# Four sums of weight blocks moved from VectorE to GpSimd in a two-layer diffusion trunk

## The chip, the cores and the metric

The kernel runs on one core of one Trainium2 chip. The metric is device time in microseconds of one execution, the median of several; less is better. The engines of the core are TensorE (PE: matmuls; PEld: its weight loads), VectorE (DVE), ScalarE (ACT), GpSimd (POOL) and SyncE (SP), which issues the DMAs.

## What is computed

Two layers of a diffusion backbone over 640 tokens (512 latent tokens on a grid, 128 context tokens) of 1024 channels. Each layer is a half-step SwiGLU FFN, a mixing stage (neighbourhood attention, pooling, short convolution, merged by gates) and a second FFN. Each of them starts with an RMSNorm, shifted and scaled by an adaLN projection of a conditioning vector. So there are four FFNs, and the change is in them:

```python
def swiglu(h, w_gate, w_up, w_down):
    return (jax.nn.silu(h @ w_gate) * (h @ w_up)) @ w_down

def trunk_layer(x, mod, lp, attend):
    h = modulate(rmsnorm(x, lp['g_ffn1']), m[0], m[1])
    x = x + 0.5 * m[2] * swiglu(h, lp['w_ffn1_gate'], lp['w_ffn1_up'], lp['w_ffn1_down'])
    ...
    x = x + m[5] * (merged @ lp['w_out'])
    h = modulate(rmsnorm(x, lp['g_ffn2']), m[6], m[7])
    x = x + 0.5 * m[8] * swiglu(h, lp['w_ffn2_gate'], lp['w_ffn2_up'], lp['w_ffn2_down'])
    return x, k, v
```

## The kernel before

**Splitting.** All matmuls are made of two-part numbers: a weight block or operand is copied to a rounded high part (hi, on ACT, line 310, tile wh for weights) and the rest is subtracted (lo, on VectorE, line 313, tile wl). One product of 128 channels is three matmuls: hi x hi, lo x hi and hi x lo (mm3, lines 305 to 307). `split` does this for activations (nhi, nlo; gh, gl for the gated activations), `w_part` for weights.

**Units.** An FFN has 22 columns of 128 hidden channels, in chunks of 8, 8 and 6. The first two columns of an FFN are multiplied as they are (`whole`); each of the other 20 is a *unit*: gate and up weights (with the two halves of the tokens) are multiplied in seven products of a Strassen-like scheme in the place of eight. A unit's weights come by three DMAs into three buffers of the ring RAW (four buffers): raw with both halves of the gate, a11 with half of up in its lower 512 columns, a12 with the other half in its upper 512. Four sums of 128x512 blocks complete them (`add`, line 386):

- sum 1: upper part of a11 = the two halves of raw
- sum 2: lower part of sm = the two parts of a11
- sum 3: upper part of sm = lower part of sm + upper part of a12
- sum 4: lower part of a12 = lower part of a11 + upper part of raw

Then a11, sm, a12 (1024 wide) and the lower part of raw (512 wide) are split into weight tiles of the ring HL (four pairs). sm is the one buffer of the ring SUM. TensorE takes the four tiles in this order: a11 for products B11 and T1, sm for T2 and B22, a12 for T3 and `prod_b`, raw for T4. Each product is four times three matmuls of 320 columns. Three results are saved from their bank by ACT (`hold`, a copy f<-b, line 310), three are added to a saved one by VectorE (`plus`, line 901), one of which, n22 after T3, must be done before T4 may write its bank. Then come silu, f x f (line 873) and the split into gh and gl. After a chunk's units the down weights are multiplied (`dn`, whole 1024-wide tiles without sums), and VectorE adds the result to x (line 799).

**Starts of an FFN.** `norm_b` makes the operand's rows: squares (line 651) and their sum on ACT and VectorE, the power -1/2 on GpSimd (line 671), scaling (line 695, 740) and split of each row of 128 channels. TensorE follows the rows with the `whole` columns. Then the forms T1 to T4 of the operand are computed, 1280 wide, and split (nhi, nlo). The gated activations gh and gl reuse memory that these forms are read from.

**adaLN.** The projections for later norms are made on VectorE in the meantime, as products of 512 with a running sum (line 573), and paced by the weight tiles that TensorE is done with.

**Order.** The order of all instructions is written out beforehand by a planner (`Sched`): processes ask for an engine with a cost (`DVE(n)`, `POOL(n)`, `ACT(n)`, `PE(n, m)`), for buffers of a ring, or for events, and the planner gives an engine to whichever request can start first, by its priority if two can. Each engine then runs its own list in that order; waits between engines are semaphores that follow the data. What a process asks for between two instructions, such as the HL slot between sums 1 and 2, places its next instruction in the plan, but is no wait of that instruction on the chip.

The lists that the change touches are those of VectorE and GpSimd (lines 386, 400, 408, 410 and 417). GpSimd otherwise runs the power of the norms (line 671), some memsets, and small products of the mixing stage (lines 1252, 1258, 1259, 1269, 1332).

Of the kernel before, what the change touches and what calls it, by code (L numbers as in the profile page):

```python
# [11 lines left out]
ALU = mybir.AluOpType  # L12
# [167 lines left out]
def DVE(n, m=1):  # L180
    return ("dve", 0.1 + m * 0.05 + n / 960)


def POOL(n):
    return ("pool", 0.16 + n * 0.0021)
# [82 lines left out]
def body(ctx: ExitStack, tc: tile.TileContext, a, outs):  # L268
    nc = tc.nc
# [100 lines left out]
    def w_part(hl, i, src, n, nk):  # L370

        hi, lo = [t[:, :n] for t in hl]
        yield ACT(n)
        copy(hi, src)
        yield DVE(n)
        sub(lo, src, hi)
        cnt["split"] += 1
        S.set(w_ev[i], (i, hl, *[t.rearrange("p (k c) -> p k c", k=nk) for t in (hi, lo)]))

    def w_split():  # L380
        def nxt():
            tile_no[0] += 1
            return tile_no[0] - 1

        def add(out, in0, in1):
            nc.vector.tensor_tensor(out=out, in0=in0, in1=in1, op=ALU.add)

        prio = S.cur.prio
        for i0, nk, ncol in pieces:
            raw = yield raw_ev[i0]  # L390
            if nk:
                hl = yield HL
                yield from w_part(hl, nxt(), raw[:, :nk * ncol], nk * ncol, nk)
                S.give(RAW, raw)
                continue
            a11 = yield raw_ev[i0 + 1]
            a12 = yield raw_ev[i0 + 2]
            lo, hi = slice(0, 512), slice(512, 1024)

            yield DVE(512)  # L400
            add(a11[:, hi], raw[:, hi], raw[:, lo])
            hl = yield HL
            p1 = S.spawn(w_part(hl, nxt(), a11, 1024, 8), prio)

            def part_b():

                sm = yield SUM
                yield DVE(512)
                add(sm[:, lo], a11[:, hi], a11[:, lo])
                yield DVE(512)  # L410
                add(sm[:, hi], sm[:, lo], a12[:, hi])
                hl = yield HL
                return sm, S.spawn(w_part(hl, nxt(), sm, 1024, 8), prio)

            def part_c():

                yield DVE(512)
                add(a12[:, lo], a11[:, lo], raw[:, hi])
                hl = yield HL
                return S.spawn(w_part(hl, nxt(), a12, 1024, 8), prio)  # L420

            sm, p2 = yield from part_b()
            p3 = yield from part_c()
            yield p1
            S.give(RAW, a11)
            yield p2
            S.give(SUM, sm)

            hl = yield HL
            yield from w_part(hl, nxt(), raw[:, lo], 512, 4)  # L430
            S.give(RAW, raw)
            yield p3
            S.give(RAW, a12)
# [1531 lines left out]
    def main():  # L1965
        S.spawn(prep(), 0)
        es = ExitStack()
        fp = es.enter_context(tc.tile_pool(name="first", bufs=1))
        for j in range(4):
            S.give(FIRST, fp.tile([128, 2048], F32, name=f"wf{j}"))  # L1970
        nt_ev = Ev()
        xe, ops = start_norms(0, 0, nt_ev)
        S.set(
            nt_ev,
            (
                [fp.tile([128, 4, 320], F32, name=f"nf{j}") for j in range(4)],
                [fp.tile([128, 4, 320], F32R, name=f"b{s}") for s in "hl"],
            ),
        )
        done = S.spawn(ada_first(first), 1)  # L1980
        S.spawn(load(xe), 2)
        S.spawn(w_split(), w_prio)
        close = closer(es, [done])
        for l in range(L):
            more = l + 1 < L
            op, _ = yield from ffn(l, 0, ops, close, lambda: start_norms(l, 1), False, l == 0)
            ops, close = yield from mix(l, op, lambda ev: start_norms(l, 2, ev))
            ops, close = yield from ffn(l, 1, ops, close, (lambda ev: start_norms(l + 1, 0, ev)) if more else None, more, False)
# [89 lines left out]
```

## Time and profile before

| | |
|---|---|
| runs shown | 2751.22, 2753.77, 2752.55 us |
| median | 2752.55 us |
| profiled execution | 2751.35 us |
| its span in the profile | 2749.6 us |
| TensorE busy | 2704.8 us (98% of the span) |
| VectorE busy | 2092.8 us (76%) |
| ScalarE busy | 1276.6 us (46%) |
| GpSimd busy | 125.6 us (5%) |

The profile is one execution. Times are microseconds from the start of the span unless marked ns. A row of the timeline is start, duration, engine, line of the kernel, operation, what is written <- what is read, shape, xcount where neighbours are merged, and in brackets the idle time of the engine before it and what ended it. Instructions of one engine are pipelined, so the next can start a little before the last has ended. Matmul durations overlap; two matmuls of 320 columns start some 0.147 us apart.

### The profile page before, as it was taken

How to read it: one execution, taken by the hardware profiler on the slowest of the kernel's cores; microseconds unless marked ns; L12 is line 12 of the kernel's file. 1: busy time of each engine (PE TensorE's matmuls, PEld its weight loads, DVE VectorE, ACT ScalarE, POOL GpSimd, SP SyncE). 2: the span in 40 equal slices, each digit the busy share in tenths (PEclk: the TensorE clock that was granted, in tenths of full speed). 3: DMA queues.
4: the chain of work that ended last, by engine and by line, in shares of the span. 5: the costliest groups of instructions: out<-in, count | busy, mean ns of one | idle time of the engine just before them, and what ended most of it. 6: DMA issues, size and time to landing. Idle time of an engine off the chain costs nothing.

```text
span 2749.6 us, 48276 instructions
## 1 busy us (share of the span) xinstructions
PE 2704.8 (98%) x19068; PEld 2679.2 (97%) x19068; DVE 2092.8 (76%) x4164; ACT 1276.6 (46%) x2312; POOL 125.6 (5%) x217
## 2 busy tenths in 40 slices
PE   7999999999999999999999999999999999999999
PEld 6999999999999999999999999999999999999999
DVE  7998976776677799988688686768766768847564
ACT  5525244895322463443464252558943225524342
POOL 0000000530000000000000000004200000000000
PEclk9999999999999999999999999999999999999999
DMA  5453523232444235353324233323234441222222
GB/s 220 142 166 102 167 95 109 89 99 74 134 135 149 75 97 167 108 160 112 104 77 138 78 109 111 98 91 108 71 97 143 138 135 47 77 92 77 93 70 85
DMA packets 123186, 304.91 MB, mean 111 GB/s; under 512 B 15696, under 2 KB 23888, under 8 KB 121936
## 3 DMA queue, kind: packets, MB, share of 16 engines
q1 hardware_dynamic: 122960, 301.83, 33.9%
q8 instruction: 149, 2.44, 0.4%
q14 instruction: 77, 0.63, 0.1%
HBM read 298.11 MB, written 3.67 MB: 110 GB/s over the span
## 4 chain that ended last, share of the span: by engine, by line
PE 92%; ACT 3%; DVE 3%; issue 1%; DMA 1%; POOL 0%; SPq 0%; DVEq 0%; POOLq 0%
PE b L305 29%; PE b L307 29%; PE b L306 29%; ACT nhi L310 1%; PE b L1466 1%; ACT t L719 1%; DVE wl L313 1%; DMA wf<-in_wm_dram 1%; PE b L1378 1%; PE b L1377 0%; PE b L1373 0%; DVE nlo L313 0%; PE b L1372 0%; PE b L1395 0%; DVE t L695 0%
## 5 line engine op out<-in xcount | busy, mean ns | idle before, releaser
L305 PE MATMUL b<-nhi,wh 128*128 128x320 f32 (+2 forms) x3584 | 1111.8, 310 | 8.0 <-ACT nhi L310 4.0
L306 PE MATMUL b<-nhi,wl 128*128 128x320 f32 (+2 forms) x3584 | 1107.2, 309 | 0.2 <-DVE wl L313 0.2
L307 PE MATMUL b<-nlo,wh 128*128 128x320 f32 (+2 forms) x3520 | 1087.9, 309 | 3.3 <-DVE nlo L313 3.2
L310 ACT ACTIVATE wh<-raw 128x1024 fp32r<-128x1024 f32 (+2 forms) x472 | 457.7, 970 | 557.2 <-PE b L307 475.7
L305 PEld LDWEIGHTS b<-nhi,wh 128*128 128x128 f32 x3584 | 673.6, 188 | 12.3 <-ACT nhi L310 6.5
L306 PEld LDWEIGHTS b<-nhi,wl 128*128 128x128 f32 x3584 | 673.7, 188 | 2.6 <-DVE wl L313 1.8
L307 PEld LDWEIGHTS b<-nlo,wh 128*128 128x128 f32 x3520 | 661.6, 188 | 6.8 <-DVE nlo L313 6.7
L313 DVE TENSOR_TENSOR wl<-raw,wh 128x1024 fp32r<-128x1024 f32 (+2 forms) x472 | 525.5, 1114 | 169.0 <-ACT wh L310 167.5
L305 PE MATMUL b<-gh,wh 128*128 128x320 f32 (+2 forms) x1424 | 440.9, 310 | 0.0
L307 PE MATMUL b<-gl,wh 128*128 128x320 f32 (+2 forms) x1424 | 440.1, 309 | 0.0
L306 PE MATMUL b<-gh,wl 128*128 128x320 f32 (+2 forms) x1424 | 439.8, 309 | 0.0
L306 PEld LDWEIGHTS b<-gh,wl 128*128 128x128 f32 x1424 | 267.8, 188 | 0.3
L305 PEld LDWEIGHTS b<-gh,wh 128*128 128x128 f32 x1424 | 267.7, 188 | 0.3
L307 PEld LDWEIGHTS b<-gl,wh 128*128 128x128 f32 x1424 | 267.8, 188 | 0.3
L799 DVE SCALAR_TENSOR_TENSOR x<-b,mh,x 128x128 f32<-128x128 f32 (+3 forms) x288 | 117.3, 436 | 160.2 <-PE b L307 160.1
L573 DVE CUSTOM_DVE_ANT_0 junk<-wm,cs,part 128x512 bf16<-128x512 f32 x256 | 191.7, 749 | 21.0 <-ACT cs L539 9.1
L310 ACT ACTIVATE f<-b 128x320 f32<-128x320 f32 x240 | 104.6, 438 | 216.2 <-PE b L307 214.0
L573 DVE CUSTOM_DVE_ANT_0 junk<-wm,cs,bm 128x512 bf16<-128x512 f32 x256 | 191.4, 748 | 14.0 <-DMA wm<-in_wmod_dram 7.7
L901 DVE TENSOR_TENSOR f<-f,b 128x320 f32<-128x320 f32 x240 | 112.2, 483 | 107.6 <-PE b L307 102.7
L305 PE MATMUL b<-wh,nhi 128*128 128x256 f32 x480 | 138.2, 288 | 0.4 <-DVE nhi L313 0.4
L306 PE MATMUL b<-wh,nlo 128*128 128x256 f32 x480 | 134.5, 280 | 2.1 <-DVE nlo L313 2.1
L307 PE MATMUL b<-wl,nhi 128*128 128x256 f32 x480 | 134.2, 280 | 0.0
(209 smaller groups left out, 3355.1 us busy)
## 6 DMA issues: line engine op xcount, KB each, us to landing
raw<-in_w_dram SPq DMA_DIRECT2D x280, 512.0 KB, 3.4
wm<-in_wmod_dram SPq DMA_DIRECT2D x256, 256.0 KB, 3.1
raw<-in_w_dram SPq DMA_DIRECT2D x160, 256.0 KB, 2.8
raw<-in_w_dram SPq DMA_DIRECT2D x32, 384.0 KB, 3.1
B<-in_rpb_dram SPq DMA_DIRECT2D x16, 640.0 KB, 4.1
wf<-in_wm_dram SPq DMA_DIRECT2D x8, 1024.0 KB, 12.0
cs<-in_crow_dram SPq DMA_DIRECT2D x20, 256.0 KB, 4.9
x<-in_xT_dram SPq DMA_DIRECT2D x4, 640.0 KB, 8.7
```

Of the source, the lines that this page charges most:

```text
L305: nc.tensor.matmul(out, lhsT=l2[0], rhs=r2[0], start=first, stop=False, skip_group_check=more)
L306: nc.tensor.matmul(out, lhsT=l2[1], rhs=r2[0], start=False, stop=False, skip_group_check=more)
L307: nc.tensor.matmul(out, lhsT=l2[0], rhs=r2[1], start=False, stop=last, skip_group_check=more)
L310: nc.scalar.activation(out=out, in_=in_, func=AF.Copy, scale=scale)
L313: nc.vector.tensor_tensor(out=out, in0=in0, in1=in1, op=ALU.subtract)
L573: nc.vector.tensor_tensor_reduce(out=junk, in0=t, in1=cs[:, g, 512 * hf:512 * hf + 512] if wide else cs[:, g], scale=1.0, scalar=start, op ...
L719: nc.scalar.activation(out=t[:, c0:c1], in_=t[:, c0:c1], func=AF.Identity, scale=gs[:, 1, d, g:g + 1], bias=M[:, 24 + d, g:g + 1])
L799: nc.vector.scalar_tensor_tensor(out=x[:, d, s], in0=bank[:, c0:c1], scalar=col[:, d, g:g + 1], in1=x[:, d, s], op0=ALU.mult, op1=ALU.add)
L901: nc.vector.tensor_tensor(out=t, in0=t, in1=bank[:, :320], op=ALU.add)
L1378: nc.tensor.matmul(out, lhsT=v, rhs=pt[1][:, :n], start=False, stop=last)
L1466: nc.tensor.transpose(bank[:, 128 * i:128 * i + 128], P[h, j][:, 128 * s:128 * s + 128], ident)
```

## The change

The helper `add` issues its tensor_tensor on GpSimd in the place of VectorE, and the four requests to the planner ask for GpSimd. Nothing else is changed: the same additions of the same blocks in the same program order.

```diff
@@ -383,7 +383,7 @@
         def add(out, in0, in1):
-            nc.vector.tensor_tensor(out=out, in0=in0, in1=in1, op=ALU.add)
+            nc.gpsimd.tensor_tensor(out=out, in0=in0, in1=in1, op=ALU.add)
@@ -397,7 +397,7 @@
-            yield DVE(512)
+            yield POOL(512)
             add(a11[:, hi], raw[:, hi], raw[:, lo])
             hl = yield HL
@@ -405,16 +405,16 @@
                 sm = yield SUM
-                yield DVE(512)
+                yield POOL(512)
                 add(sm[:, lo], a11[:, hi], a11[:, lo])
-                yield DVE(512)
+                yield POOL(512)
                 add(sm[:, hi], sm[:, lo], a12[:, hi])
...
-                yield DVE(512)
+                yield POOL(512)
                 add(a12[:, lo], a11[:, lo], raw[:, hi])
```

The planner's costs of the two, for n columns:

```python
def DVE(n, m=1):
    return ("dve", 0.1 + m * 0.05 + n / 960)

def POOL(n):
    return ("pool", 0.16 + n * 0.0021)
```

## Rows read from the trace of the kernel before

**Rows 1.** The page, span and first part: busy time, share, instructions.

```profile
span 2749.6 us, 48276 instructions
PE 2704.8 (98%) x19068; PEld 2679.2 (97%) x19068; DVE 2092.8 (76%) x4164; ACT 1276.6 (46%) x2312; POOL 125.6 (5%) x217
```

**Rows 2.** Stretches with units: length, busy of PE, PEld, DVE, ACT, POOL; clock, DMA.

```profile
68.00:137.00 69.00, 69.00 (x471) 68.76 (x470) 63.42 (x111) 40.28 (x68) 0.00 (x0) 1.00 0.41 140
186.00:285.00 99.00, 99.00 (x677) 99.00 (x677) 88.02 (x166) 46.13 (x76) 0.00 (x0) 1.00 0.34 107
...
990.00:1056.00 66.00, 65.08 (x442) 64.84 (x443) 61.43 (x108) 38.52 (x66) 0.00 (x0) 1.00 0.45 146
1105.00:1204.00 99.00, 99.00 (x677) 99.00 (x676) 88.04 (x164) 46.70 (x76) 0.00 (x0) 1.00 0.33 108
...
1427.00:1494.00 67.00, 65.98 (x447) 65.25 (x446) 59.43 (x101) 38.33 (x64) 0.00 (x0) 1.00 0.39 129
```

**Rows 3.** The same stretches, the sums of line 386 alone: length, DVE busy (instructions).

```profile
68.00:137.00 69.00, 13.50 (x20) 1.00 0.41 140
186.00:285.00 99.00, 19.05 (x29) 1.00 0.34 107
...
990.00:1056.00 66.00, 13.60 (x20) 1.00 0.45 146
1105.00:1204.00 99.00, 19.64 (x29) 1.00 0.33 108
...
1427.00:1494.00 67.00, 13.59 (x20) 1.00 0.39 129
```

**Rows 4.** The starts of the second to fourth FFN, columns as in rows 2.

```profile
954.00:992.00 38.00, 34.13 (x216) 31.40 (x216) 34.61 (x59) 28.19 (x56) 1.03 (x3) 1.00 0.13 40
1393.00:1430.00 37.00, 33.26 (x215) 31.27 (x215) 33.07 (x57) 24.82 (x50) 0.85 (x1) 1.00 0.13 38
2311.00:2349.00 38.00, 34.12 (x216) 31.38 (x216) 34.60 (x59) 28.18 (x56) 0.85 (x1) 1.00 0.11 37
```

**Rows 5.** Waits of TensorE, whole span: us in total, times, longest.

```profile
PE b L305 <- ACT f L310: 4.0, 3, 1.6
...
PE b L307 <- DVE nlo L313: 3.2, 8, 0.8
```

**Rows 6.** Timeline of VectorE at the start of the second FFN.

```profile
982.27 0.69 DVE L386 TENSOR_TENSOR sum<-raw 128x512 f32<-128x512 f32 x1
...
984.20 1.22 DVE L313 TENSOR_TENSOR wl<-raw,wh 128x1024 fp32r<-128x1024 f32 x1
...
986.74 2.88 DVE L313 TENSOR_TENSOR nlo<-sg,nhi 128x1280 fp32r<-128x1280 f32 x2
```

**Rows 7.** Timeline of ACT in the same place.

```profile
989.71 0.83 ACT L310 ACTIVATE gh<-t 128x320 fp32r<-128x320 f32 x2 [2.88 <-issue]
990.44 0.75 ACT L310 ACTIVATE f<-b 128x320 f32<-128x320 f32 x2
```

**Rows 8.** GpSimd's products by line: count, ns min/median/max, first and last start, forms.

```profile
L1332 POOL TENSOR_TENSOR nlo<-nlo,ones x48: 457/732/1604, 499.3 to 1965.0; 64x256 fp32r<-64x256 f32 x32, 64x128 fp32r<-64x128 f32 x16
...
L1252 POOL TENSOR_TENSOR t<-sga x30: 608/616/1455, 514.1 to 1951.2; 128x256 f32<-128x256 f32 x30
```

**Rows 9.** Timeline of GpSimd and of VectorE, both from 510.4 to 513.

```profile
510.50 2.94 POOL L1332 TENSOR_TENSOR nlo<-nlo,ones 64x256 fp32r<-64x256 f32 x3 [2.87 <-ACT nlo L310]
...
510.63 1.68 DVE L313 TENSOR_TENSOR wl<-raw,wh 128x1024 fp32r<-128x1024 f32 x1
```

**Rows 10.** Timeline of VectorE in one unit of the last FFN.

```profile
2511.38 0.48 DVE L901 TENSOR_TENSOR f<-f,b 128x320 f32<-128x320 f32 x1
2511.78 1.22 DVE L313 TENSOR_TENSOR wl<-raw,wh 128x1024 fp32r<-128x1024 f32 x1
...
2521.02 0.49 DVE L901 TENSOR_TENSOR f<-f,b 128x320 f32<-128x320 f32 x1 [2.73 <-PE b L307]
```

**Rows 11.** Timeline of GpSimd at the start of the second FFN.

```profile
962.81 0.85 POOL L671 TENSOR_TENSOR small<-small,nhalf 128x3 f32<-128x3 f32 x1 [18.60 <-DVE small L667]
```

## The prediction

> **What bounds the kernel now.** I read the first part of the page first: TensorE is busy for 2704.8 us of a span of 2749.6 us, so at most 44.8 us can be won by anything that only feeds it better [rows 1]. The second look is a table of stretches: five of the stretches in which units run, at the starts of the chunks with most adaLN work. There VectorE is the engine behind TensorE: 63.42 of 69 us, 88.02 of 99, 61.43 of 66, 88.04 of 99, 59.43 of 67 [rows 2], and the sums that move are 13.5 to 13.6 us of it where 20 of them run and 19 to 19.6 us where 29 run [rows 3]. TensorE nevertheless has no gap in three of these five, and about 1 us in each of the other two, which begin with the end of an FFN's start. So in steady state the sums cost nothing now: VectorE runs them in a hole.
>
> Third, the FFN starts, the one place where TensorE waits and units are at work: 38.00 - 34.13 = 3.87 us, 37.00 - 33.26 = 3.74 us and 38.00 - 34.12 = 3.88 us of idle [rows 4], 11.5 us together. The list of waits names them: three waits of 305 for ACT's copy of a bank (f, line 310), 4.0 us, and waits for the lower parts nlo, 3.2 us over eight places, of which those in these stretches are part [rows 5]. The timeline of one start tells why ACT is late: VectorE makes three sums of the first unit back to back from 982.27, reaches the unit's first wl at 984.20, then three 1280-wide lower parts, the last of which ends at 986.74 + 2.88 = 989.62 [rows 6]. ACT's gh reuses the memory that this last part reads: it starts at 989.71, two of them take 0.83 us, and the copy of the bank that TensorE waits for stands behind them [rows 7]. Three sums of about 0.69 us, 1.93 us together, are thus on the path that ends in the 4.0 us.
>
> **The change, part by part.** It moves 4 additions per unit, 320 in the kernel (80 units), from VectorE's queue to GpSimd's, and the planner is told 1.24 us (0.16 + 512 x 0.0021) for each instead of 0.68. No DMA moves.
>
> *Price of one sum on GpSimd.* The trace has no 128x512 addition there. Its nearest rows are the products of line 1332: the shortest, a 64x128 one, takes 457 ns, the median, a 64x256 one, 732 ns [rows 8]. That is 275 ns for 128 columns; 256 more make 1.28 us, an estimate. The square of line 1252, 256 wide, takes 616 ns, twice which is 1.23 us. I take 1.28; four are 5.1 us of a unit of 12.3 us (84 matmuls at 99.00 / 677 = 0.146 us [rows 2]). GpSimd is otherwise empty in units [rows 2], so its own time is covered.
>
> *What it does to VectorE beside it.* The trace shows that the two engines do not run side by side for every operation. At 510.50 GpSimd starts three products; at 510.63 VectorE starts a wl of two SBUF inputs and takes 1.68 us [rows 9] where such a one takes 1.22 [rows 10]: 0.46 us longer, until 0.14 us before the first product's end (510.50 + 0.73). The second product, begun behind it, is the long one of that line: its maximum is 1.60 us against 0.73 [rows 8]. So a sum may hold off VectorE's next two-input operation for 1.28 - 0.14 = about 1.15 us, more than the 0.69 us that it takes off VectorE. The operations that would be held off are wl, f x f, gl and the adaLN products; line 901 reads one input from a bank, and I assume that it runs through.
>
> [...]
>
> *Steady units: taken at 0.* With every hold-off in full, the five stretches need 63.42 - 13.50 + 20 x 1.15 = 72.9 us of 69, 88.02 - 19.05 + 29 x 1.15 = 102.3 of 99, then 70.8 of 66, 101.8 of 99 and 68.8 of 67 [rows 2, 3]: over by 3.9, 3.3, 4.8, 2.8 and 1.8, 16.6 us together. Against that stands line 901: three per unit at 0.4 us from start to start (2511.38 to 2511.78 [rows 10]), 1.2 us per unit, 15 x 0.4 = 6 us or 21 x 0.4 = 8.4 us per stretch, under which a sum can run free; that is more than each excess. In a unit without adaLN work VectorE waits 2.73 us before line 901 [rows 10], more than 4 x (1.15 - 0.69) = 1.84. I expect the sums to start early: sum 1 waits only for its block and for the last reader of the buffer it writes, sums 2 and 3 for their loads, sum 4 for the wl of the unit before; ACT needs the first much later. What must not be late is line 901: the product T4 follows T3 after prod_b, 12 matmuls or 1.76 us, and 901 takes 0.49 us, so it has some 1.2 us to spare. The bounds are 0 and +16.6 us.
>
> *FFN starts: -4.0 us, of 0 to -4.0.* The three sums leave VectorE (1.93 us), so the last lower part can end 1.9 us sooner than 989.62, and ACT's gh and copy with it. The longest of the three waits is 1.6 us [rows 5], below 1.93: all 4.0 us go. What is late next is nothing in that place: T1 runs on. The cover of this is that the sums are over before the lower parts begin. In the code, sum 2 is asked for only after a slot of HL, which is why VectorE has it at 982; but no semaphore of the addition stands for that slot, so GpSimd, in order, may run it as soon as its queue reaches it. The power of line 671 at 962.81 stands ahead of it [rows 11]; behind that it can run in some 4 us.
>
> *The norm rows of these starts: +2.1 us, of 0 to +3.5.* The first sum of an FFN will now run when its block lands, in the middle of the lower parts nlo for which TensorE waits [rows 5], instead of at a quiet moment. It can hold off one of them by up to 1.15 us; I take 0.7 for each of three starts. The start of the first FFN has no wait of TensorE on units; taken at 0.
>
> *GpSimd's queue.* The power of line 671 is the only thing there that a norm waits for. It takes 0.85 us [rows 11]; a sum ahead of it would delay it by 1.28 us at most. In the plan the sums of a unit start when the norm is done, or long before; taken at 0, bounds 0 and +1.3 per start.
>
> The sum: -4.0 + 2.1 = -1.9 us. The profiled execution took 2751.35 us and would take 2749.5; it stands 1.2 us under the median of the runs, so I forecast 2752.55 - 1.9 = 2750.7 us, a change that cannot be told from none: 0.2%, or 5.5 us, is about what a measurement of this kernel can tell.
>
> **The rivals.** *First: VectorE with the hold-offs becomes the bound of the units.* It decides where line 901 comes later than its 1.2 us, which needs adaLN products in the unit, so in the five stretches of [rows 2]. For it: after the move VectorE's queue is 94 to 98% full there even with line 901 free (72.9 - 6 of 69, 102.3 - 8.4 of 99, and so on), the order is fixed beforehand, and the plan knows of no hold-off. Against it: the hole before line 901 and TensorE's unbroken run now. All of it without cover costs 16.6 us: 2750.7 + 16.6 = 2767.3 us, slower.
>
> *Second: sums 2 to 4 of the first unit don't run early but where they ran, at 982.* Then they meet lower parts of 1.4 us back to back, and hold them off by 3 x 1.15 = 3.45 us instead of using 1.93: +1.5 us at each of three starts in the place of the 4.0 us won. 2752.55 + 4.5 + 2.1 = 2759.2 us, slower. It decides on what the plan puts into GpSimd's queue ahead of them.
>
> *Third: the freed 2.7 us of VectorE per unit are worth more.* The plan may put other rows of the norm forward; of the 11.5 us of idle at the starts, 7.5 are left beside the 4.0. If the 2.1 us of loss don't come and 2 us of these go too: 2752.55 - 6.0 = 2746.5 us, faster.
>
> **How the numbers follow.** The forecast 0.47, the first rival 0.25, the second 0.13, the third 0.15. Faster by over 0.2% (below 2747.0) only in the third: 0.15. Slower by over 0.2% (above 2758.1) in the first two: 0.38. Within it 0.47. The range takes in the second rival and the first up to its full price with the norm's upper bound, and below some 1.5 us more than the third: 2745 to 2770 us.
>
> **What would show it.** Right: no wait of 305 for ACT's f at the FFN starts, sums of 1.3 us on GpSimd with a tail to some 2.4 us, wl, gl and f x f with a tail of up to 1.15 us more, TensorE without a gap inside units. First rival: gaps of TensorE before T4, ended by line 901, in the stretches of [rows 2]. Second: the first unit's sums 2 to 4 lie among the 1280-wide lower parts. The forecast is wrong if a sum takes over 2 us alone, or if line 901 is held off as well.

## The result and the profile after

| kernel | median of its runs, us | lowest to highest | span of the profiled execution, us |
|---|---|---|---|
| before | 2753.07 | 2751.22 to 2753.77 | 2749.6 |
| after | 2785.84 | 2783.46 to 2786.51 | 2783.8 |

After to before is 1.0120, 95% interval 1.0107 to 1.0133: slower by 33 us. The forecast of 2750.7 us and the whole range of 2745 to 2770 us lie below it.

The page after: span, and the busy time of each engine (us, share, instructions).

```profile
span 2783.8 us, 48529 instructions
PE 2721.8 (98%) x19068; PEld 2686.6 (97%) x19068; DVE 2123.0 (76%) x3844; ACT 1264.3 (45%) x2312; POOL 634.7 (23%) x537
```

Against [rows 1]: 320 instructions went from VectorE to GpSimd, and yet VectorE's busy time rose by 30.2 us. GpSimd's rose by 509 us. TensorE is busy 17 us longer with the same 19068 matmuls, and idle 17 us longer; both will have a cause below.

The first two lines are sums on GpSimd, the next two VectorE's product f x f with who waited for it (us in total, times), and the last is its line 901 (ns shortest/median/longest).

```profile
L386 POOL TENSOR_TENSOR raw<-raw x80: 1272/1481/2477, 39.8 to 2711.0; 128x512 f32<-128x512 f32 x80
L386 POOL TENSOR_TENSOR sum<-sum,raw x80: 1263/1638/2162, 42.5 to 2715.2; 128x512 f32<-128x512 f32 x80
...
L873 DVE TENSOR_TENSOR f<-f,f x160: 476/484/1584, 83.3 to 2738.7; 128x320 f32<-128x320 f32 x160
...
  ACT gh L310: 102.5, 52
...
L901 DVE TENSOR_TENSOR f<-f,b x240: 471/486/490, 79.2 to 2736.5; 128x320 f32<-128x320 f32 x120
```

A sum alone takes 1.27 us, half of them 1.48 us and more, the longest 2.48. f x f, two operands in SBUF, has a tail up to 1.58 us where it took 0.48; line 901, one operand in a bank, has none. And ACT's copy gh of the product waits 102.5 us for f x f, where it waited 2.9 us in the kernel before.

Waits of TensorE, whole span (us in total, times, longest), to be read against [rows 5].

```profile
PE b L305 <- ACT f L310: 12.0, 19, 2.4
...
PE b L305 <- DVE f L901: 6.6, 6, 1.9
PE b L305 <- ACT nhi L310: 5.5, 8, 1.4
```

The three waits for ACT's f are now nineteen. For line 901 TensorE did not wait before; all six of its waits lie in the first units behind the starts of FFNs 2 to 4. These three lines (4.0 us before for nhi) and wl (1.9 us instead of 0.2) are some 18 us more than before; to see the rest I took, from the start times of the matmuls, all time from one start to the next beyond an estimate of the usual spacing (0.146 us for 320 columns, 99.00 / 677 in [rows 2]; 0.120 and 0.173 us for the few of 256 and 384, whose medians from start to start before are 0.118 and 0.173), where it is over 60 ns, and summed it between the same matmuls of each kernel. The columns with other names are experiments, told below. Each profile, and so each column, is of one execution, and those of one sum, of halves and, below, of the first units with four sums lie 1.9, 4.4 and 4.1 us above the median of their kernel.

| us lost to TensorE | before | after | old order | new order, sums on VectorE | memsets | planned later | sum 1 only | halves |
|---|---|---|---|---|---|---|---|---|
| starts of FFNs 2 to 4 (940 to 1000, 1380 to 1437, 2300 to 2357 of before) | 24.2 | 31.9 | 27.1 | 25.8 | 21.5 | 26.0 | 34.6 | 29.9 |
| first units behind the four starts (66 to 140, 1000 to 1060, 1437 to 1497, 2357 to 2420) | 0.8 | 11.7 | 11.4 | 6.5 | 2.2 | 14.6 | 2.6 | 8.6 |
| the other units, with the last matmuls ahead of attention (140 to 480, 1060 to 1380, 1497 to 1850, from 2420) | 7.3 | 21.9 | 17.5 | 8.0 | 6.9 | 8.9 | 7.3 | 7.2 |

The rest of the kernel is 38 us in before and in after. So the 33 us are 7.7 + 10.9 + 14.6 us, in three places. The way from VectorE to TensorE is not the same in all of them.

**The other units.** Timeline after, in a unit of the last FFN, without adaLN work (start, us, engine, line; in brackets the idle time before it and what ended it). GpSimd, VectorE, ACT and TensorE in turn.

```profile
2713.80 1.32 POOL L386 TENSOR_TENSOR sum<-raw 128x512 f32<-128x512 f32 x1 [1.32 <-DMA raw<-in_w_dram]
2715.20 2.16 POOL L386 TENSOR_TENSOR sum<-sum,raw 128x512 f32<-128x512 f32 x1
...
2713.89 2.32 DVE L313 TENSOR_TENSOR wl<-raw,wh 128x1024 fp32r<-128x1024 f32 x1
2716.13 1.58 DVE L873 TENSOR_TENSOR f<-f,f 128x320 f32<-128x320 f32 x1
...
2717.74 0.47 ACT L310 ACTIVATE gh<-f 128x320 fp32r<-128x320 f32 x1 [2.73 <-DVE f L873]
2718.12 0.75 ACT L310 ACTIVATE f<-b 128x320 f32<-128x320 f32 x2
...
2718.59 0.41 PE L305 MATMUL b<-nhi,wh 128*128 128x320 f32 x1 [0.53 <-ACT f L310]
```

The second sum starts 0.09 us before wl: wl takes 2.32 us instead of 1.22. The third sum starts behind the second, finds wl running and takes 2.16 us; now f x f stands still beside it, 1.58 us instead of 0.48. The two engines take turns, and two hold-offs of 1.10 us follow one another: f x f ends 2.2 us later than it would. ACT has gh at the head of its queue and is idle for 2.73 us; behind gh stands the copy of a bank, which line 305 wants. TensorE waits 0.53 us. Waits of this kind, 0.3 to 0.7 us, stand at many places of the units.

**The start of the first FFN.** Timeline after: GpSimd, VectorE, SP's queue, ACT, TensorE.

```profile
68.50 1.80 POOL L386 TENSOR_TENSOR sum<-raw 128x512 f32<-128x512 f32 x1 [0.69 <-DMA raw<-in_w_dram]
...
66.58 5.07 DVE L313 TENSOR_TENSOR nlo<-nf,nhi 128x1280 fp32r<-128x1280 f32 x2
...
71.72 0.33 SPq L552 DMA_DIRECT2D wm<-in_wmod_dram  x1
72.10 0.90 SPq L533 DMA_DIRECT2D cs<-in_crow_dram  x2
...
77.78 1.06 ACT L539 ACTIVATE cs<-cs 128x1024 f32<-128x1024 f32 x1 [3.41 <-DMA cs<-in_crow_dram]
78.74 0.42 ACT L310 ACTIVATE f<-b 128x320 f32<-128x320 f32 x1
...
79.21 0.42 PE L305 MATMUL b<-nhi,wh 128*128 128x320 f32 x1 [2.41 <-ACT f L310]
```

Two lower parts of 1280 columns take 5.07 us instead of the 2.88 of [rows 6]. The load wm waits 5.7 us in SP's queue for the second of them to end; the loads cs stand behind it (before, cs went out at 68.72, ahead of wm). ACT waits 3.41 us for cs, the copy of the bank stands behind that, and TensorE waits 2.41 us.

**The starts of the second and third FFN.** Here wm stands ahead of cs in the kernel before too, and it waits 4.0 us for a lower part instead of 2.9 at the second: two of 1280 columns take 3.99 us, held off by the first sum of the second unit. Timeline after: ACT, VectorE, TensorE.

```profile
1008.34 1.06 ACT L539 ACTIVATE cs<-cs 128x1024 f32<-128x1024 f32 x1 [2.57 <-DMA cs<-in_crow_dram]
...
1009.79 0.87 DVE L313 TENSOR_TENSOR gl<-t,gh 128x320 fp32r<-128x320 f32 x1 [2.52 <-ACT gh L310]
...
1011.11 0.41 PE L305 MATMUL b<-nhi,wh 128*128 128x320 f32 x1 [1.87 <-DVE f L901]
```

ACT waits for cs, gh stands behind cs, VectorE's gl waits for gh, line 901 stands behind gl, and TensorE waits for line 901. At the third FFN ACT waits 2.16 us for cs and TensorE 1.55 us for line 901. With the fourth FFN counted, the three waits for ACT's f of the kernel before, 4.4 us by matmul starts, are gone from these starts, and three waits for line 901, 4.6 us by matmul starts, have come.

**The granted clock.** Table of stretches after (length; busy and count of PE, PEld, DVE, ACT, POOL; granted clock; DMA share; GB/s).

```profile
79.00:84.00 5.00, 4.79 (x22) 4.79 (x23) 3.00 (x5) 3.15 (x6) 2.80 (x3) 0.66 0.34 132
...
965.00:970.00 5.00, 3.54 (x14) 2.75 (x15) 5.00 (x10) 4.88 (x11) 0.00 (x0) 0.79 0.35 104
970.00:975.00 5.00, 5.00 (x33) 5.00 (x33) 2.90 (x8) 3.40 (x7) 0.48 (x1) 0.87 0.13 53
```

Behind that wait of 2.41 us the granted clock falls for a while to 0.50 (from 81 to 83 us): 22 matmuls in 5 us, where the kernel before has 34 in the same 5 us at 1.00:

```profile
79.00:84.00 5.00, 5.00 (x34) 4.76 (x33) 5.00 (x8) 4.39 (x7) 0.00 (x0) 1.00 0.29 105
```

It happens at four places after (80.5, 967.9, 1012.3 and 1418.5 us), each behind waits of TensorE, and at none of these before. One such fall takes (1 - 0.66) x 5 = 1.7 us of full clock, or (0.21 + 0.13) x 5 = 1.7 us in the other two rows. The four falls are at most 6.8 of the 17 us by which TensorE's busy time rose. Busy time rises beside waits at full clock too: by 1.3 us in the stretch shown with the rivals below (100.33 us, clock 1.00, against 99.00).

### The profile page after: what moved, and what is told of

Its sections match the earlier page's. It is cut to its first block, busy times and chain, and to the rows that moved or that the text cites. A ratio compares the mean times of both kernels' runs of the same rounds, so it can differ in the third digit from the quotient of the medians.

```text
span 2783.8 us, 48529 instructions
## 1 busy us (share of the span) xinstructions
PE 2721.8 (98%) x19068; PEld 2686.6 (97%) x19068; DVE 2123.0 (76%) x3844; ACT 1264.3 (45%) x2312; POOL 634.7 (23%) x537
## 5 line engine op out<-in xcount | busy, mean ns | idle before, releaser
L313 DVE TENSOR_TENSOR wl<-raw,wh 128x1024 fp32r<-128x1024 f32 (+2 forms) x472 | 592.6, 1257 | 152.6 <-ACT wh L310 151.9
L386 POOL TENSOR_TENSOR raw<-raw 128x512 f32<-128x512 f32 x80 | 119.1, 1489 | 650.7 <-DVE wl L313 631.7
L573 DVE CUSTOM_DVE_ANT_0 junk<-wm,cs,part 128x512 bf16<-128x512 f32 x256 | 211.2, 825 | 20.7 <-ACT cs L539 8.9
L573 DVE CUSTOM_DVE_ANT_0 junk<-wm,cs,bm 128x512 bf16<-128x512 f32 x256 | 216.2, 845 | 12.2 <-DMA wm<-in_wmod_dram 6.4
L671 POOL TENSOR_TENSOR small<-small,nhalf 128x3 f32<-128x3 f32 (+1 forms) x12 | 12.0, 1000 | 743.7 <-DVE small L667 743.7
L386 POOL TENSOR_TENSOR sum<-raw 128x512 f32<-128x512 f32 x80 | 126.5, 1581 | 184.7 <-DMA raw<-in_w_dram 86.8
```

The costliest lines, as they stand in the source:

```text
L313: nc.vector.tensor_tensor(out=out, in0=in0, in1=in1, op=ALU.subtract)
L386: nc.gpsimd.tensor_tensor(out=out, in0=in0, in1=in1, op=ALU.add)
L573: nc.vector.tensor_tensor_reduce(out=junk, in0=t, in1=cs[:, g, 512 * hf:512 * hf + 512] if wide else cs[:, g], scale=1.0, scalar=start, op ...
L671: nc.gpsimd.tensor_tensor(out=rs[:, :nb], in0=rs[:, :nb], in1=nhalf[:, :nb], op=ALU.pow)
```

## The experiments

The theory from this profile (A in the expectations): hold-offs between VectorE and the sums make f x f late, ACT's gh waits for it, and the copy of a bank stands behind gh. The rivals: the new order itself (B), and the latency of sums of 1.3 us (C). Every ratio is to the kernel before in the same set of runs (its median was between 2752.05 and 2752.36 us), with its 95% interval.

**Old order, sums on GpSimd.** The order of every engine's work is that of before; the four additions alone go to GpSimd.

```diff
             yield DVE(512)
...
-            nc.vector.tensor_tensor(out=out, in0=in0, in1=in1, op=ALU.add)
+            nc.gpsimd.tensor_tensor(out=out, in0=in0, in1=in1, op=ALU.add)
```

> The order of every engine as in the kernel before (the planner is asked for VectorE with its old cost); only the instruction of each sum is GpSimd's. Theory A (two-input operations of VectorE and the sums shut each other out, f x f comes late, ACT's gh waits for it and the copy of a bank for TensorE stands behind gh): the hold-offs are there in this order too, 2765 to 2800 us, waits of 305 for ACT's f well over the 4.0 us of before. Theory B (the plan with VectorE relieved is a worse order by itself): 2748 to 2757 us. Theory C (four sums of 1.3 us in a row bring the weight tiles late): 2765 to 2800 us, but the waits are for wl or wh.

2776.08 us, 1.0089 (1.0074 to 1.0104). Waits of TensorE:

```profile
PE b L305 <- ACT f L310: 12.3, 27, 1.5
```

With the old order 24 of the 33 us are there, and the wait for ACT's f is as long as after. The new order is not the main cause.

**New order, sums on VectorE.** The planner believes in GpSimd, the instruction is VectorE's.

```diff
             yield POOL(512)
...
-            nc.gpsimd.tensor_tensor(out=out, in0=in0, in1=in1, op=ALU.add)
+            nc.vector.tensor_tensor(out=out, in0=in0, in1=in1, op=ALU.add)
```

> The order of every engine as in the changed kernel, but each sum is VectorE's instruction, at its place in the new plan. No GpSimd sum, so no hold-off. Theory A: most of the 32.8 us goes, 2748 to 2760 us. Theory B: 2775 to 2795 us. Theory C: 2748 to 2760 us.

2761.61 us, 1.0035 (1.0022 to 1.0048), and TensorE waits:

```profile
PE b L306 <- DVE wl L313: 6.3, 7, 1.1
PE b L305 <- ACT f L310: 2.2, 1, 2.2
```

So the order by itself costs about 9.6 us when VectorE has to do what the plan took off it. ACT's gh waits for f x f here too, 68.3 us in all, and the other units lose hardly more than before (8.0 us, 7.3 before): a wait of gh costs only where the copy behind it comes too late for TensorE. The 2.2-us wait for ACT's f is the one at the start of the first FFN: it comes with wm ahead of cs in the new order, also without a sum on GpSimd. (That order alone is not enough: the memsets below have it too, with wm issued at 68.35 instead of 69.88 here, and a wait of 0.3 us.) The expectation of A was a little too low.

**Memsets in place of the sums.** GpSimd writes the same block for about as long, in three memsets, and reads nothing. The additions are left out.

```diff
-            nc.gpsimd.tensor_tensor(out=out, in0=in0, in1=in1, op=ALU.add)
+            nc.gpsimd.memset(out, 0.0)
+            nc.gpsimd.memset(out, 0.0)
+            nc.gpsimd.memset(out[:, 0:64], 0.0)
```

> The changed kernel with each sum replaced on GpSimd by three memsets of the same block (512, 512 and 64 columns, about 1.2 us by the 152 ns for 64 and 298 ns for 240 columns in the trace): the addition itself is left out, GpSimd is as busy, but reads nothing of SBUF. Theory A: without a read no hold-off, 2745 to 2757 us, and f x f, wl and gl have their old longest durations. Theory B: 2775 to 2795 us. Theory C: 2770 to 2795 us, less only by what the loads no longer hold up.

2747.52 us, 0.9982 (0.9972 to 0.9991): 38 us less than after, and 4.5 us less than before. The same product as above:

```profile
L875 DVE TENSOR_TENSOR f<-f,f x160: 482/485/494, 79.5 to 2702.8; 128x320 f32<-128x320 f32 x160
```

Nothing is held off, and the order of after is then even a gain. So it is not the plan that costs, and not GpSimd's writing: f x f takes up to 1.58 us beside sums and at most 0.49 us beside memsets, which write the same block and read nothing of SBUF. The memsets do not wait for loads as the sums do (sums 2 and 3 wait 158.1 us in all for theirs in the kernel after), so they alone do not exclude C, the latency of sums. But in the kernel after a single instruction of another engine waited for a sum (us, times):

```profile
  ACT wh L310: 3.3, 1
```

C falls by this, and by the halves below, where the sums take longer and less is lost.

**The product planned later.** The planner is told that f x f ends 1.2 us later than it computes, so the order leaves room between f x f and gh.

```diff
             nc.vector.tensor_tensor(out=s, in0=s, in1=u, op=ALU.mult)
+            S.cur.end += 1.2
             yield from split(g2[0][:, slot, half.s], g2[1][:, slot, half.s], s, 320)
```

> The changed kernel; the planner is told that the product f x f is known 1.2 us later, so that ACT's gh is placed later in ACT's queue, behind the copies of banks. The hold-offs stay. Theory A with ACT's queue as the carrier: the waits of 305 for ACT's f fall from 12.0 us to under 5, those for line 901 stay near 6.6, in all 2765 to 2778 us. Theory A with line 901 alone as the carrier, B and C: 2781 to 2790 us.

2769.78 us, 1.0065 (1.0050 to 1.0080).

```profile
PE b L306 <- DVE wl L313: 4.5, 7, 1.7
PE b L305 <- ACT f L310: 3.9, 3, 3.4
PE b L305 <- DVE f L902: 3.6, 6, 1.3
```

15 to 16 us are back. The table by place is clearer than the time: in the other units the loss goes from 14.6 to 1.6 us. There, then, f x f, gh and the copy behind it are the way to TensorE. The first units behind the starts are not helped (11.7 to 14.6 us); one wait of 3.4 us for ACT's f is the one at the first start.

**One sum of the four.** Only the first sum of each unit is on GpSimd, the other three on VectorE.

```diff
-            yield DVE(512)
+            yield POOL(512)
             add(a11[:, hi], raw[:, hi], raw[:, lo])
```

> The kernel before, with only the first of a unit's four sums on GpSimd, in all 80 units. Theory A in proportion to the number of hold-offs: a quarter of the 33 us or less, +2 to +12 us, and ACT's wait for f x f between 10 and 40 us. Theory C (it is four sums in a row on GpSimd, 1.3 us each, that make the weight tiles late; a single one does nothing): within 2 us of the kernel before.

2760.41 us, 1.0030 (1.0020 to 1.0040): a quarter of the loss, as expected. But the place is another one: all of it is at the starts of FFNs 2 to 4 (24.2 to 34.6 us), and the units lose about 2 us. Timeline at one start (GpSimd, VectorE, TensorE), and the table of stretches around it:

```profile
952.12 1.30 POOL L394 TENSOR_TENSOR raw<-raw 128x512 f32<-128x512 f32 x1 [8.28 <-DVE wl L313]
...
952.20 1.57 DVE L313 TENSOR_TENSOR nlo<-sg,nhi 128x320 fp32r<-128x320 f32 x1
...
955.37 0.42 PE L305 MATMUL b<-nhi,wh 128*128 128x320 f32 x1 [0.70 <-ACT nhi L310]
```

```profile
950.00:955.00 5.00, 4.34 (x27) 3.59 (x25) 5.00 (x8) 1.64 (x3) 1.30 (x1) 1.00 0.16 54
955.00:960.00 5.00, 3.71 (x14) 2.92 (x15) 5.00 (x11) 4.91 (x11) 0.00 (x0) 0.79 0.38 113
960.00:965.00 5.00, 5.00 (x33) 5.00 (x33) 2.72 (x7) 3.22 (x6) 0.62 (x1) 0.87 0.11 44
```

The sum of the first unit holds off a lower part by 1.09 us (1.57 against 0.48). The next wait of TensorE, for ACT's nhi, is 0.70 us where it was 0.22 us before. Behind these waits the clock falls, (0.21 + 0.13) x 5 = 1.7 us. The clock falls so at four places of this kernel, all at the starts (957.9, 1401.6, 1435.7 and 2323.2 us). And the first sum of the second unit holds off two lower parts of 1280 columns, which take 2.88 us in [rows 6]; TensorE's waits for ACT's f behind them were 4.0 us before:

```profile
988.33 3.98 DVE L313 TENSOR_TENSOR nlo<-sg,nhi 128x1280 fp32r<-128x1280 f32 x2
```

```profile
PE b L305 <- ACT f L310: 7.3, 3, 2.7
```

By matmul starts, the 10.4 us are 2.0 us in waits for rows, 3.3 us in the waits for ACT's f, and some 5 us behind the four falls. So this run is no proof of A in the units; it measures the starts. In the other units a single hold-off per unit loses nothing (7.3 us as before).

**Only the first units of FFNs 2 to 4**, all four of their sums on GpSimd, and then the second to fourth alone (`u` counts the units, `i` a unit's sums; the plan has GpSimd's cost for those alone):

```diff
+            e = nc.gpsimd if u in (21, 41, 61) else nc.vector
...
+            e = nc.gpsimd if u in (21, 41, 61) and i > 1 else nc.vector
```

> The kernel before, with the four sums of only the first unit of the second, third and fourth FFN on GpSimd; the sums of the other 77 units stay on VectorE. Theory A (a VectorE operation with two operands in SBUF stands still while a sum runs, so f x f comes late, ACT's gh waits for it and the copy of a bank behind gh waits too): at these three places there is no f x f yet, so the price is the normalization rows behind the first sum only; the three waits of L305 for ACT f at the FFN starts go (about -4.0 us) and the rows there cost about +2; together 2748 to 2753 us. Theory B' (the FFN starts gain nothing, the sums there only come late): 2753 to 2758 us.

> The same, but the first sum of those three units stays on VectorE too: only sums two to four are on GpSimd. Theory A: the normalization rows have no sum beside them, so the -4.0 us of the FFN starts stay and the +2 go: 2747 to 2750 us. Theory B': no gain, 2752 to 2757 us.

2752.94 us, 1.0005 (0.9996 to 1.0014), and 2751.37 us, 0.9995 (0.9987 to 1.0004). Stretch at the same place, first with all four sums, then with three:

```profile
956.00:961.00 5.00, 4.08 (x17) 3.29 (x17) 5.00 (x11) 4.87 (x11) 0.00 (x0) 0.74 0.51 156
```

```profile
956.00:961.00 5.00, 4.58 (x27) 3.83 (x27) 4.83 (x12) 4.89 (x11) 0.00 (x0) 1.00 0.32 105
```

With the first sum on VectorE the clock stays at 1.00, 27 matmuls against 17. In neither kernel does TensorE wait for ACT's f at these starts any more. The gain that I forecast there is real at two of them (1.4 us each in matmul starts), but the start of the third FFN gives it back: a wait of 1.5 us for line 901 and one of 0.9 us for wl are new. No sum runs beside that place; line 901 is late because ACT waits 2.9 us for the load cs (2.0 us before), with gh behind it and VectorE's gl waiting for gh. So the load is what is late next. The time with three sums lies between the two expectations, and neither kernel can be told from no change.

**Each sum in two halves** of 256 columns.

```diff
-            nc.gpsimd.tensor_tensor(out=out, in0=in0, in1=in1, op=ALU.add)
+            w = out.shape[1] // 2
+            for h in range(2):
+                s = slice(h * w, h * w + w)
+                nc.gpsimd.tensor_tensor(out=out[:, s], in0=in0[:, s], in1=in1[:, s], op=ALU.add)
```

> The changed kernel, with each sum as two halves of 256 columns on GpSimd (about 0.7 us each, estimated from 1.27 us for 512 columns). Theory A: what an f x f can lose to one instruction is halved, but a VectorE operation in a queue of eight halves can still meet two; 2765 to 2783 us if the longest single hold-off counts, 2783 to 2795 us if the total time with GpSimd reading counts. Theory C (latency of the sums): 2785 us or more, since eight instructions take longer than four.

2760.93 us, 1.0034 (1.0022 to 1.0046): some 24 us less than after, better than either end I gave.

```profile
L876 DVE TENSOR_TENSOR f<-f,f x160: 472/486/1029, 82.9 to 2718.4; 128x320 f32<-128x320 f32 x160
```

One hold-off is now 0.55 us. Over all instructions of VectorE, the time above the mean of the same operation and shape before sums to 196 us with halves and 233 us after: nearly the same total, more often and shorter. In the other units the loss is gone (7.2 us against 7.3 before). What decides is how late a single chain can get, not how much time VectorE loses: two hold-offs in a row are 1.1 us here and 2.2 us after.

**Halves, and the product planned 0.6 us later.** Both edits together.

> The kernel with each sum as two halves of 256 columns on GpSimd, whose planner is also told that f x f is known 0.6 us later than it has it (one hold-off by a half). Theory A: the remaining waits of ACT for f x f (54.7 us with halves) shrink again and about half of the 8.6 us that the halves still cost go: 2753 to 2759 us. Theory A' (what is left with halves is VectorE's own time lost): 2759 to 2763 us.

2759.19 us, 1.0026 (1.0016 to 1.0035). ACT's gh waits 28.0 us for f x f instead of 54.7, and the time is within 2 us of that with halves alone: the border of both expectations, so it tells little. What is left is at the first units behind the starts (7.7 us against 0.8), not in the others.

**The plan reserves VectorE for the sum.**

```diff
-            yield POOL(512)
+            yield ("dve", 1.28)
```

> The changed kernel, whose plan puts each sum at 1.28 us on VectorE instead of on GpSimd; the instruction itself still goes to GpSimd. The plan then knows that VectorE stands still beside a sum, but it does not know of how long GpSimd waits in its turn. Theory A (the loss is f x f, gh and the copies of banks coming later than the plan has them): the list of every engine is ordered with that room in it, and the time comes down to 2758 to 2775 us. Theory B (an order with VectorE relieved is worse by itself): about 2770 to 2780 us, since the order is tight on VectorE again but the hold-offs stay.

2817.31 us, 1.0233 (1.0218 to 1.0248): both theories missed. The waits for ACT's f grow to 45.0 us at 49 places and gh's wait for f x f to 146.7 us. A plan in which VectorE is blocked 5.1 us per unit is worse than one which doesn't know of it; why the order comes out so stays open.

**Does it go through ACT?** The copy gh moves from ACT to VectorE, with the sums on GpSimd and, as a base, on VectorE.

```diff
-            yield from split(g2[0][:, slot, half.s], g2[1][:, slot, half.s], s, 320)
+            yield DVE(320)
+            nc.vector.tensor_copy(out=g2[0][:, slot, half.s], in_=s)
+            yield DVE(320)
+            sub(g2[1][:, slot, half.s], s, g2[0][:, slot, half.s])
```

> The changed kernel, with the copy gh of the products f x f on VectorE instead of on ACT (160 copies of 320 columns): ACT then never waits for f x f. Theory A with ACT's queue as the carrier: the waits of ACT for f x f (102.5 us) go and TensorE's waits for ACT's f (12.0 us) with them; if the hold-offs do nothing else, the difference to the kernel before with the same move is under 15 us instead of 33 us. Theory A' (the hold-offs make VectorE itself late, whoever does gh): the difference stays at 25 to 35 us and shows as waits for VectorE's f and wl.

> The kernel before (all sums on VectorE), with the copy gh on VectorE instead of on ACT: what that move costs by itself, the base for the run with the sums on GpSimd. Per unit two copies of 320 columns more on VectorE, two less on ACT; VectorE is busy 2182 us of 2750 before, and 160 copies of some 0.3 us (estimated below the 0.48 us of f x f, which has two operands) are 50 us more: 2750 to 2765 us by either theory.

2783.46 us, 1.0114 (1.0099 to 1.0130), against 2751.55 us, 0.9997 (0.9988 to 1.0006). (VectorE's 2182 us before, in the expectation here and in that of the banks, is a slip: the page has 2092.8.) ACT does not wait for f x f, and the difference is still 32 us. With the sums on GpSimd (waits of TensorE; the copy) and with the sums on VectorE (the copy):

```profile
PE b L305 <- DVE f L904: 17.3, 19, 2.0
...
L875 DVE CAST gh<-f x160: 320/1303/1466, 85.8 to 2742.2; 128x320 fp32r<-128x320 f32 x160
```

```profile
L875 DVE CAST gh<-f x160: 318/327/331, 85.2 to 2705.8; 128x320 fp32r<-128x320 f32 x160
```

The copy, with a single operand, is held off too: its median is 1.30 us beside sums and 0.33 us without. So the run made a new victim and did not tell the two ways apart.

So the copies of the banks were moved instead, which read PSUM:

```diff
         def hold(bank, ev):
...
-            yield ACT(320)
-            copy(t, bank[:, :320])
+            yield DVE(320)
+            nc.vector.tensor_copy(out=t, in_=bank[:, :320])
```

> The changed kernel, with the copies of the banks into f (240 of 320 columns, one operand, out of PSUM) on VectorE instead of on ACT: they can no longer stand behind gh in ACT's queue. Theory A through ACT's queue: the difference to the kernel before with the same move falls under 15 us (from 33 us), although ACT's gh still waits for f x f. Theory A' (VectorE itself late): the difference stays at 25 us or more, with waits of TensorE for VectorE's f.

> The kernel before (all sums on VectorE), with the copies of the banks on VectorE instead of on ACT: the base for the run with the sums on GpSimd. By the 0.33 us that a copy of 320 columns took on VectorE, 240 of them add some 80 us to 2182 us of work in 2750 us: 2752 to 2770 us by either theory.

2837.27 us, 1.0309 (1.0293 to 1.0324), against 2757.96 us, 1.0021 (1.0012 to 1.0030). Waits of TensorE with the sums on GpSimd, then with them on VectorE:

```profile
PE b L305 <- DVE f L896: 40.5, 58, 4.0
```

```profile
PE b L305 <- DVE f L896: 3.0, 3, 1.0
```

The copy itself is not held off (0.481 us mean beside sums, 0.490 without), but it stands in VectorE's queue behind what is. The difference grows from 33 to 79 us. That corrects theory A: ACT's queue is not the fault, it is the better of two carriers. The lateness is VectorE's; it reaches TensorE by whichever in-order queue a bank's release shares with a held-off result, directly on VectorE or one step behind it on ACT.

**Both harmless edits together**: sums two to four of the three first units on GpSimd, and gh on VectorE.

> The kernel before, with the sums two to four of only the first unit of the second, third and fourth FFN on GpSimd, and gh on VectorE: the two edits that measured 0.9995 and 0.9997 by themselves. If the -4 us of the FFN starts are real and gh on VectorE is free: 2747 to 2750 us; if both are nothing: 2751 to 2753 us.

2750.80 us, 0.9994 (0.9985 to 1.0003): 1.5 us, and no more than the two edits by themselves promised. No version with the sums computed on GpSimd beats the kernel before by more than a measurement can tell.

## Why the prediction was wrong, step by step

*Price of a sum: right.* 1.28 us was forecast, alone it takes 1.27 us. *Hold-off: right.* 1.15 us was forecast, 1.10 us is measured (2.32 - 1.22 and 1.58 - 0.48). *Line 901 runs through: right* (471/486/490 ns).

*FFN starts, -4.0 us: right in mechanism, too large.* Behind the power of line 671, sums 2 to 4 of the first unit run back to back on GpSimd from 975.35 to 979.44 us (the forecast was some 4 us), and none of the starts of FFNs 2 to 4 has a wait of 0.1 us or more for ACT's f. What is late next is what I took for nothing: the load cs and behind it line 901, and wl. In the changed kernel the waits for line 901 take back the 4.4 us that the waits for ACT's f gave; in the kernel with three sums one of 1.5 us is left. There the gain is 1.0 us in the time, not told from none; with memsets, where nothing is held off, the starts gain 24.2 - 21.5 = 2.7 us.

*Norm rows, +2.1 us: the wait right, the term mis-sized.* The sum does hold off one lower part per start, and TensorE waits 0.5 us more for it, near the 0.7 that I took. But behind that wait the granted clock can fall (0.79 and 0.87 in two stretches of 5 us), 1.7 us at a time. Only the first sum on GpSimd makes the starts 10.4 us dearer in matmul starts, some 5 us of it behind four such falls and 3.3 us by the second unit's sum, which the prediction did not count; after, it is 7.7 us in all, with two falls. Rows 4 show a clock of 1.00 in these stretches, and the prediction did not ask whether one more wait would end that.

*GpSimd's queue at 0: right.* The power of line 671 runs ahead of the sums (974.51, then 975.35). The sum behind it holds off line 674, which reads its result (1.65 us instead of 0.55), and TensorE waits 0.12 us for that.

*Steady units at 0: the step that failed.* "What must not be late is line 901 [...] it has some 1.2 us to spare." Line 901 was late at six waits (6.6 us), all in the first units behind the starts of FFNs 2 to 4. In the other units, where 14.6 us were lost, something else was late: gh on ACT, which waits for f x f, with the copy of a bank behind it. The prediction had read this pair, gh and behind it the copy, at the FFN start [rows 7], and did not ask for it in the units. And the hold-offs of a unit were summed and set against the idle time of VectorE, as if they were spread; two of them fall on neighbouring instructions, 2.2 us in a row. The 1.2 us to spare were worked out for line 901; the pair's own slack was some 2.2 - 0.53 = 1.7 us in the example above, an estimate from its wait of 0.53 us. The halves, with 1.1 us in a row, are free there, which fits; no run set the slack itself.

*The start of the first FFN, taken at 0:* 4 us of the 10.9 in the first units. There the plan puts wm ahead of cs in SP's queue, and a held-off lower part holds wm. The wait comes with the order alone too (2.2 us), but not with the same order and memsets (0.3 us): it needs a late VectorE, whatever makes it late.

*The rivals.* The first, with 0.25, had the direction: VectorE's hold-offs do decide. Its sign, gaps ended by line 901, is there only behind the starts. By matmul starts its five stretches lose 4.6, 2.8, 5.4, 3.4 and 2.6 us, close to the 3.9, 3.3, 4.8, 2.8 and 1.8 of its sum; another 14 us are lost in units that it left out, with less adaLN work or none, and in the rows of the normalization. But its reason, a VectorE that is full, does not hold. The second stretch of [rows 2], 186 to 285 us of before, after and with halves (columns as there):

```profile
191.90:293.72 101.82, 100.33 (x678) 99.03 (x677) 96.05 (x142) 44.64 (x76) 43.91 (x27) 1.00 0.32 105
```

```profile
190.99:289.99 99.00, 99.00 (x678) 99.00 (x676) 91.37 (x141) 45.25 (x76) 60.12 (x54) 1.00 0.35 108
```

After, VectorE is busy 96.05 of 101.82 us, hold-offs included; that would have fitted into the 99.00 us of before, so it is not full. With halves GpSimd runs longer, VectorE is busy 91.37 of 99.00 us, and nothing is lost. The agreement in size is taken as chance. The second is excluded: the sums ran early. The third is seen with memsets alone, 4.5 us faster: freed VectorE time is worth that, if it really is free.

What stays open: what makes the clock fall behind the waits at one start and not at another, how the 24 us of the old order and the 9.6 us of the new one add to 33 (they need not), and why a plan that reserves VectorE does worse.

## What to carry to other kernels

The sums moved to GpSimd, which read SBUF, ran not beside VectorE's two-operand work but in turn with it (f x f and wl took 1.10 us more where they stood still beside a sum of 1.27 us). Before such a move, count the longest run of hold-offs on neighbouring instructions against the slack of every result in it, and cut the moved instruction into smaller ones if it must move. Follow each late result into the in-order queue of the engine that consumes it, and see what stands behind the consumer: that is where TensorE's wait came from here. Where TensorE already has several short waits, price another one by what the granted clock may do behind it as well (1.7 us a fall here).

## What was not expected of the hardware

TensorE's granted clock fell behind short waits: with one sum on GpSimd to 0.79 over 5 us, behind waits of 0.34, 0.70, 0.33 and 0.16 us that followed one another, and in the kernel after to 0.66 over 5 us (0.50 from 81 to 83 us), behind a single one of 2.41 us. 14 and 22 matmuls in 5 us followed, where the kernel before has 22 and 34. It is not sure to fall: at the start of the fourth FFN after, waits of 0.70, 0.34, 0.15 and 0.42 us pass at full clock.

```profile
2340.00:2345.00 5.00, 3.34 (x16) 2.02 (x15) 5.00 (x9) 4.11 (x9) 0.00 (x0) 1.00 0.28 95
```

A copy on VectorE with one operand, SBUF to SBUF, took 1.30 us beside sums on GpSimd and 0.33 us without; the same size of copy out of PSUM took 0.48 us either way. And a sum on GpSimd is held off in its turn: it took 2.16 us where it had found a wl running, and up to 2.48 us elsewhere.
